# Cross-covariance attention: Q and K of five units loaded as 8 KB rows, with masked copies of Q

## The chip, the cores and the metric

The kernel runs on one core of a Trainium2 chip. Its time is the device time of one execution in microseconds (us), 127.44 at the median of three runs (127.34 to 127.64). A core has five engines with queues of their own: TensorE (PE, with its weight loads shown apart as PEld), VectorE (DVE), ScalarE (ACT), GpSimd (POOL) and SyncE (SP, which here only issues transfers). Sixteen DMA engines move data between HBM and the on-chip memory SBUF, which has 128 partitions; matrix products land in PSUM.

## The reference

Batch 8, 12 heads, 512 positions, dimension 64, all float32. Q and K are normalised along the positions, their 64 x 64 product goes through a softmax, and V is multiplied by it:

```python
Q_norm = Q / (np.linalg.norm(Q, axis=-2, keepdims=True) + 1e-10)
K_norm = K / (np.linalg.norm(K, axis=-2, keepdims=True) + 1e-10)
attn = np.einsum('bhnd,bhne->bhde', Q_norm, K_norm)
attn = np.exp(attn - np.max(attn, axis=-1, keepdims=True))
attn = attn / (np.sum(attn, axis=-1, keepdims=True) + 1e-10)
return np.einsum('bhnd,bhde->bhne', V, attn).astype(np.float32)
```

Each of Q, K, V and the output is 12.58 MB.

## The kernel before, in words

The 96 heads are cut into 12 units of 8 heads (`S = 12`), two units make a pair (`W = 6`). A unit's Q is one tile of 128 partitions x 2,048 floats (1 MB), and so is its K; a pair's V is two such tiles.

**How rows lie in a tile.** For Q and K (`Qf`, `Kf`, L168) a row of 16 positions of one head, 4 KB, goes to a partition: 32 partitions hold one head, 128 hold four, and the tile has two such groups side by side (`r`), so a load of a whole tile (L221) takes 256 rows of 4 KB. For V (`Vu`, L170) a row is 32 positions, 8 KB, a head has 16 partitions, and a tile is 128 rows.

**One unit.** `cast_qk` (L244) makes bf16 copies of Q and K in which the two heads of a partition lie beside each other, `square` (L249) squares them. `grams` (L258) multiplies K and Q: 64 matmuls of 32 rows by 128 columns, so that two heads share a product of 128 x 128 of which the two diagonal blocks are used. `sums` (L265) adds the squares over the partitions with 8 matmuls, `fold` (L272) and `norms` (L276) bring the sums to where they are needed, `powers` (L280) takes them to the power -1/2. `scale_k` (L286), `logits` (L290, four transposes), `scales_q` (L294, one call for each half of the partitions) and `exps` (L300) give the exponentials, `normalise` (L304) the softmax in bf16.

**One pair.** `cast_v` (L316) makes bf16 of V, `vtrans` (L321) transposes it on PE, `vcopy` (L328) copies it from PSUM, `outs` (L334) multiplies it by the softmax, and `ocopy` (L344) copies the product to an output tile, which `store` (L229) writes to HBM. The store of unit 9 is cut in four (`CUTS`, L231), of which a part of 124 rows and one of 4 rows carry 1,536 bytes a row; those of units 10 and 11 are halved (`HALF`, L233).

**The order.** Nothing is scheduled by the hardware or by the framework: `Order.run` (L100) plays the kernel through once, before it is built, with costs in us for each piece (`piece`, L397, and the calls under it), a rank for each kind of piece (`R`) and a bias for each choice of engine (`BIAS`), and so fixes the order of each engine's queue. For casts, squares and copies it also picks the engine. All loads of Q, K and V but the first two of K, and all stores, stand in SP's queue, in one order. SP issues in that order: where an issue has to wait for its buffer, all later ones wait behind it. Eight transfers can be under way at a time, since an issue also waits for the landing of the eighth before it.

**Buffers.** Seven tiles for Q and K as they come (`NB["qk"]`, L177), three for V, two each for the bf16 copies and squares, six for outputs. A load of Q or K waits until the tile seven places earlier has been cast.

Of the kernel before, what the change touches and what calls it, by code (L numbers as in the profile page):

```python
# [18 lines left out]
 'R': {'ck': 14.3601,  # L19
       'q': -46.9145,  # L20
       'sq': -4.5261,
       'sk': 21.309,
       'gr': 31.9137,
       's1': -8.269,
       'rd': 14.1273,
       'nn': -13.565,
       'pw': -22.1669,
       'kx': 16.8281,
       'lg': -36.3133,
       'qs': 14.727,  # L30
       'ex': 7.4539,
       'nm': 23.5766,
       'cv': -5.1919,
       'vt': 13.5707,
       'vc': 31.4911,
       'ou': -17.6156,
       'oc': 6.4318},
 'BIAS': {('cv', 'DVE'): 12.3272,
          ('vc', 'ACT'): 5.2627,
          ('oc', 'DVE'): 7.9654,  # L40
          ('q0', 'ACT'): -9.0842,
          ('sk', 'ACT'): 4.174,
          ('sk', 'DVE'): 5.4091,
          ('cv', 'ACT'): 0.906,
          ('cv', 'POOL'): -0.1651,
          ('ck', 'DVE'): -11.8527,
          ('ck', 'ACT'): -10.4645,
          ('ck', 'POOL'): -15.4937,
          ('oc', 'ACT'): 4.7795,
          ('sq', 'DVE'): -12.3114,  # L50
          ('sq', 'ACT'): -21.9953,
          ('q0', 'DVE'): -28.6804,
          ('q0', 'POOL'): -29.3142,
          ('vc', 'DVE'): -20.4676},
 'QK_PACE': 0.9356,
 'V_FROM': 0.0874,
 'V_PACE': 0.7666,
 'ST_LAG': 6.0835,
 'SPLIT': 3,
 'HALF': (10, 11),  # L60
 'WAKE': ('SP',),
 'CUTS': ((0, 0, 6, 0, 124), (0, 0, 6, 124, 128), (0, 6, 16, 0, 128), (1, 0, 16, 0, 128))}

D = 64
T = 32
# [86 lines left out]
def kernel(  # L152
# [13 lines left out]
    FINE = PAR["FINE"]  # L166

    Qf, Kf = (x.rearrange("b h (p t) d -> (b h p) (t d)", t=TT).rearrange("(w r e p) x -> w e p r x", r=2, e=2, p=128)  # L168
              for x in (Q, K))
    Vu = V.rearrange("b h (p t) d -> (b h p) (t d)", t=T).rearrange("(w r p) x -> w r p x", r=2, p=128)  # L170
# [9 lines left out]
    qmp = ctx.enter_context(tc.tile_pool(name="qmp", bufs=NB["qm"]))  # L180
    sqp = ctx.enter_context(tc.tile_pool(name="sqp", bufs=NB["sq"]))
# [31 lines left out]
    def load_qk(s, x, c):  # L213
        w, e = divmod(s, 2)
        if (s, x) not in qk32:
            qk32[s, x] = qp.tile([128, T, D], F32, name="qk32")
        issue = nc.scalar if (s, x) == (0, 1) and PAR["ACTQ"] else nc.sync
        o = qk32[s, x][:, cols(c)].rearrange("p t d -> p (t d)")
        i = (Qf, Kf)[x][w, e]
        if c is None:  # L220
            issue.dma_start(out=o.rearrange("p (r x) -> p r x", r=2), in_=i)  # L221
        else:
            issue.dma_start(out=o, in_=i[:, c])
# [17 lines left out]
    def heads(c):  # L241
        return slice(0, 2) if c is None else slice(c, c + 1)

    def cast_qk(eng, s, x, c):  # L244
        if (s, x) not in qkb:
            qkb[s, x] = qmp.tile([128, TT, 2, D], BF16, name="qb" if x == 0 else "kb")
        copy(eng, qkb[s, x][:, :, heads(c)], qk32[s, x][:, cols(c)].rearrange("p (r t) d -> p t r d", t=TT))

    def square(eng, s, x, c):  # L249
        if s not in sq:  # L250
            sq[s] = sqp.tile([128, 2, TT, 2, D], BF16, name="sq")
        o, i = sq[s][:, x, :, heads(c)], qkb[s, x][:, :, heads(c)]
        if eng == "ACT":
            nc.scalar.activation(o, i, AF.Square)  # L254
        else:
            nc.vector.tensor_tensor(out=o, in0=i, in1=i, op=ALU.mult)

    def grams(s):  # L258
        gram[s] = ps_g.tile([128, HU, 4, 2 * D], F32, name="gram")
        for t in range(TT):  # L260
            for h in range(HU):
                q, k = (qkb[s, x][32 * h:32 * (h + 1), t].rearrange("p r d -> p (r d)") for x in range(2))
                nc.tensor.matmul(gram[s][:, h, 0], k, q, start=(t == 0), stop=(t == TT - 1))  # L263

    def sums(s):  # L265
        st[s] = ps_l.tile([D, 4, 2 * D], F32, name="l")
        for t in range(0, TT, 4):
            for x in range(2):
                nc.tensor.matmul(st[s][32 * x:32 * (x + 1)].rearrange("p t d -> p (t d)"), hm,  # L269
                                 sq[s][:, x, t:t + 4].rearrange("p t r d -> p (t r d)"), start=(t == 0), stop=(t == TT - 4))  # L270

    def fold(s):  # L272
        s2[s] = small.tile([D, 2 * D], F32, name="s2")
        nc.vector.tensor_reduce(out=s2[s], in_=st[s].rearrange("p t d -> p d t"), axis=mybir.AxisListType.X, op=ALU.add)  # L274

    def norms(s):  # L276
        nn[s] = ps_l.tile([128, 2 * HU], F32, name="l")
        nc.tensor.matmul(nn[s], s2[s], sel, start=True, stop=True)  # L278

    def powers(s):  # L280
        ln = small.tile([128, 2 * HU], F32, name="ln")
        r12[s] = small.tile([128, 2 * HU], F32, name="r12")
        nc.scalar.activation(ln, nn[s], AF.Ln, bias=tiny[:, 0:1])  # L283
        nc.scalar.activation(r12[s], ln, AF.Exp, scale=-0.5)  # L284

    def scale_k(s):  # L286
        kqs[s] = small.tile([128, HU, 2 * D], F32, name="kqs")
        nc.vector.tensor_tensor(out=kqs[s], in0=gram[s][:, :, 0], in1=r12[s][:, HU:, None].to_broadcast([128, HU, 2 * D]), op=ALU.mult)  # L288

    def logits(s):  # L290
        for h in range(HU):
            nc.tensor.transpose(gram[s][:, h, 1], kqs[s][:, h], ident)  # L292

    def scales_q(s, r):  # L294
        if r == 0:
            ls[s] = small.tile([128, HU, D], F32, name="ls")
        half = (LO, HI)[r]
        nc.vector.tensor_tensor(out=ls[s][half], in0=gram[s][half, :, 1, half], in1=r12[s][half, :HU, None].to_broadcast([D, HU, D]), op=ALU.mult)  # L298
# [66 lines left out]
    hm = const.tile([128, 32], BF16, name="hm")  # L365
    nc.gpsimd.memset(hm, 0.0)
    own = const.tile([128, HU], F32, name="own")
    nc.vector.tensor_reduce(out=own, in_=ident.rearrange("p (h i) -> p h i", h=HU), axis=mybir.AxisListType.X, op=ALU.add)
    nc.vector.tensor_copy(hm[:, 0:HU], own)
    sel = const.tile([D, 2 * HU], F32, name="sel")  # L370
    for x in range(2):
        nc.gpsimd.tensor_copy(sel[:, HU * x:HU * (x + 1)], ident[0:D, 32 * x:32 * x + HU])
# [6 lines left out]
    def size(key):  # L379
        n = {"gr": 128, "s1": 16, "nn": 4, "lg": 8, "vt": 8, "ou": 32}[key[0]]  # L380
        return n // 2 if key[0] == "vt" and key[-1] is not None else n

    LOCK = {"ck", "q0", "sq", "sk", "nm", "cv"}
# [11 lines left out]
    CHOICE = ("ck", "q0", "sq", "sk", "cv", "vc", "oc")  # L395
# [17 lines left out]
    def uses(i):  # L413
        s, x = divmod(i, 2)
        return every("ck" if x else "q0", s)

    last = None
    for s in range(S):
        for c in parts(s):
            for x in range(2):  # L420
                key = ("l" + "qk"[x], s, c)
                piece(key, {"DMA": 2 * X if c is None else X}, uses(2 * s + x - NB["qk"]), [last],
                      PAR["QK_PACE"] * ((s + 0.5 * (c or 0)) / S), load_qk, s, x, c)
                last = key
    SM = NB["sm"]
    for s in range(S):
        for c in parts(s):
            dve, act, tt = two(c, 0.16, 0.52), two(c, 0.18, 0.84), two(c, 0.16, 0.52)
            for x, (load, cast, sqr, rank) in enumerate((("lq", "q0", "sq", "q"), ("lk", "ck", "sk", "ck"))):
                free = [("gr", s - NB["qm"])] + every(sqr, s - NB["qm"]) if s >= NB["qm"] else []  # L430
                piece((cast, s, c), {"DVE": dve, "ACT": act, "POOL": 2 * dve}, [(load, s, c)] + free, [], R[rank] + 0.01 * s, cast_qk, s, x, c)
                piece((sqr, s, c), {"DVE": tt, "ACT": act}, [(cast, s, c), back("s1", s, NB["sq"])], [], R[sqr] + 0.01 * s, square, s, x, c)
        piece(("gr", s), {"PE": 1.2}, every("ck", s) + every("q0", s) + [back("qs", s, 1, 0), back("qs", s, 1, 1)], [], R["gr"] + 0.01 * s, grams, s)
        piece(("s1", s), {"PE": 1.2}, every("sk", s) + every("sq", s) + [back("pw", s, 1)], [], R["s1"] + 0.01 * s, sums, s)
        piece(("rd", s), {"DVE": 0.69}, [("s1", s), back("nn", s, SM)], [], R["rd"] + 0.01 * s, fold, s)
        piece(("nn", s), {"PE": 0.3}, [("rd", s)], [], R["nn"] + 0.01 * s, norms, s)
        piece(("pw", s), {"ACT": 0.52}, [("nn", s), back("qs", s, SM, 0), back("qs", s, SM, 1)], [], R["pw"] + 0.01 * s, powers, s)
        piece(("kx", s), {"DVE": 0.69}, [("gr", s), ("pw", s), back("lg", s, SM)], [], R["kx"] + 0.01 * s, scale_k, s)
        piece(("lg", s), {"PE": 0.7}, [("kx", s)], [], R["lg"] + 0.01 * s, logits, s)
        for r in range(2):  # L440
            piece(("qs", s, r), {"DVE": 0.43}, [("lg", s), back("ex", s, SM)], [("qs", s, 0)] if r else [], R["qs"] + 0.01 * s, scales_q, s, r)
        piece(("ex", s), {"ACT": 0.425}, [("qs", s, 0), ("qs", s, 1), back("nm", s, SM)], [], R["ex"] + 0.01 * s, exps, s)
# [6 lines left out]
    for w in range(W):  # L449
# [9 lines left out]
        for n, (q, f) in enumerate(turns(w)):  # L459
# [3 lines left out]
            else:  # L463
                wait = [("qs", S - 1, 0), ("qs", S - 1, 1)] + ([("vc", w, *turns(w)[n - 4])] if n >= 4 and turns(w)[n - 4][1] is not None else [])
# [57 lines left out]
```

## Time and profile before

| | |
|---|---|
| median of three runs | 127.44 us (127.34 to 127.64) |
| the profiled execution | 127.3 us, span 125.2 us |
| granted PE clock, mean | 0.875 |
| busy: PE, PEld | 79.2 us (63%), 52.6 us (42%) |
| busy: DVE, ACT, POOL | 78.9 us (63%), 84.9 us (68%), 47.5 us (38%) |
| moved by DMA | 50.59 MB, mean 404 GB/s |
| read from and written to HBM | 37.75 MB, 12.58 MB |

The span runs from the first to the last event of the profiled execution; 2.1 us of its 127.3 lie around it. The profile's slices cut the span into 40 parts of 3.13 us; a digit is the busy share in tenths. The DMA row is the mean over the 16 DMA engines. The chain is followed back from the last instruction, at each step to what released it. A line of a group shows what is written and read, with shapes, the number of instructions, busy time, mean duration in ns and the idle time ahead of it. L numbers are lines of the kernel. The trace also holds a record of each DMA packet with its time and size, and of each landing: every DMA engine that took part in a transfer tells when its share is in.

### The profile page before, as it was taken

How to read it: one execution, taken by the hardware profiler on the slowest of the kernel's cores; microseconds unless marked ns; L12 is line 12 of the kernel's file. 1: busy time of each engine (PE TensorE's matmuls, PEld its weight loads, DVE VectorE, ACT ScalarE, POOL GpSimd, SP SyncE). 2: the span in 40 equal slices, each digit the busy share in tenths (PEclk: the TensorE clock that was granted, in tenths of full speed). 3: DMA queues.
4: the chain of work that ended last, by engine and by line, in shares of the span. 5: the costliest groups of instructions: out<-in, count | busy, mean ns of one | idle time of the engine just before them, and what ended most of it. 6: DMA issues, size and time to landing. Idle time of an engine off the chain costs nothing.

```text
span 125.2 us, 4066 instructions
## 1 busy us (share of the span) xinstructions
PE 79.2 (63%) x1800; PEld 52.6 (42%) x1800; DVE 78.9 (63%) x140; ACT 84.9 (68%) x116; POOL 47.5 (38%) x40
## 2 busy tenths in 40 slices
PE   0019369873598787859637798882898879941000
PEld 0024254561474475538525455461275456630000
DVE  2043475876852989987987599993799978700000
ACT  4068594784698853998799997938958697863000
POOL 3330665382627088061806925065144810000000
PEclk9999955999657999995999999999599999997555
DMA  3999999999999999999999999999999999999993
GB/s 129 399 419 431 424 411 418 427 419 415 420 424 423 420 428 408 421 414 428 410 432 424 410 421 415 429 414 420 427 428 410 416 416 414 418 408 412 415 395 154
DMA packets 11785, 50.59 MB, mean 404 GB/s; under 512 B 888, under 2 KB 1016, under 8 KB 10232
## 3 DMA queue, kind: packets, MB, share of 16 engines
q1 hardware_dynamic: 11480, 49.29, 95.8%
q10 hardware_dynamic: 288, 1.05, 2.3%
q8 instruction: 14, 0.23, 0.7%
q14 instruction: 3, 0.02, 0.0%
HBM read 37.75 MB, written 12.58 MB: 402 GB/s over the span
## 4 chain that ended last, share of the span: by engine, by line
DMA 70%; PE 9%; ACT 5%; DVE 4%; issue 2%; SPq 1%; ACTq 0%
DMA qk<-in_Q_dram 37%; DMA out_dram<-so 17%; DMA qk<-in_K_dram 16%; ACT so L207 5%; PE po L341 3%; PE gram L263 2%; PE gram L292 1%; PE vps L326 1%; DVE kqs L288 1%; DVE qb L209 1%; PE l L269 1%; DVE ab L313 1%; DVE s L274 0%; PE l L278 0%; ACT ln L283 0%
## 5 line engine op out<-in xcount | busy, mean ns | idle before, releaser
L211 POOL TENSOR_SCALAR kb<-qk 128x2048 bf16<-128x2048 f32 (+1 forms) x13 | 23.0, 1771 | 37.8 <-DMA qk<-in_K_dram 30.9
L254 ACT ACTIVATE sq<-qb 128x2048 bf16<-128x2048 bf16 (+1 forms) x13 | 23.1, 1776 | 7.8 <-DVE qb L209 7.6
L207 ACT COPY so<-po 128x512 f32<-128x512 f32 x47 | 25.6, 584 | 3.9 <-PE po L341 2.3
L211 POOL TENSOR_SCALAR vb<-v 128x1024 bf16<-128x1024 f32 x15 | 21.4, 1444 | 13.4 <-DMA v<-in_V_dram 9.6
L341 PE MATMUL po<-ab,vt 128*32 128x128 bf16 x768 | 20.2, 232 | 6.6 <-ACT so L207 2.1
L263 PE MATMUL gram<-qb,kb 32*128 32x128 bf16 x768 | 15.5, 237 | 12.3 <-DVE qb L209 8.8
L209 DVE CAST qb<-qk 128x2048 bf16<-128x2048 f32 (+1 forms) x12 | 13.7, 1143 | 11.2 <-DMA qk<-in_Q_dram 10.7
L326 PE MATMUL vps<-ident,vb 128*128 128x128 f32 x96 | 17.3, 305 | 4.7 <-POOL vb L211 2.7
L269 PE MATMUL l<-sq,hm 128*32 128x512 bf16 x96 | 18.4, 442 | 1.7 <-ACT sq L254 1.6
L263 PEld LDWEIGHTS <-kb 32*128 32x128 bf16 x768 | 13.3, 104 | 14.4 <-POOL kb L211 10.3
L341 PEld LDWEIGHTS <-vt 128*32 128x32 bf16 x768 | 13.8, 101 | 12.4 <-issue 7.9
L209 DVE COPY vt<-vps 128x1024 bf16<-128x1024 bf16 (+1 forms) x25 | 16.5, 665 | 3.4 <-PE vps L326 3.1
L207 ACT CAST vb<-v 128x1024 bf16<-128x1024 f32 x9 | 12.1, 1341 | 8.8 <-DMA v<-in_V_dram 8.6
L254 ACT ACTIVATE sq<-kb 128x2048 bf16<-128x2048 bf16 (+1 forms) x10 | 17.3, 1733 | 0.6 <-POOL kb L211 0.6
L326 PEld LDWEIGHTS vps<-ident,vb 128*128 128x128 f32 x96 | 11.2, 151 | 8.5 <-POOL vb L211 3.2
L274 DVE TENSOR_REDUCE s<-l 64x128 f32<-64x512 f32 x12 | 8.1, 677 | 6.5 <-PE l L269 6.5
L298 DVE TENSOR_TENSOR ls<-gram,r 64x256 f32<-64x256 f32 x24 | 10.1, 420 | 2.2 <-PE gram L292 1.9
L292 PE MATMUL gram<-ident,kqs 128*128 128x128 f32 x48 | 9.0, 316 | 3.5 <-DVE kqs L288 3.0
L288 DVE TENSOR_TENSOR kqs<-gram,r 128x512 f32<-128x512 f32 x12 | 8.3, 689 | 3.7 <-ACT r L284 3.1
L313 DVE TENSOR_TENSOR ab<-ex,rb 128x512 bf16<-128x512 f32 x12 | 9.3, 773 | 0.4
L269 PEld LDWEIGHTS <-hm 128*32 128x32 bf16 x96 | 5.5, 104 | 9.4 <-issue 7.4
L292 PEld LDWEIGHTS gram<-ident,kqs 128*128 128x128 f32 x48 | 5.7, 154 | 7.4 <-DVE kqs L288 6.6
(25 smaller groups left out, 40.2 us busy)
## 6 DMA issues: line engine op xcount, KB each, us to landing
v<-in_V_dram SPq DMA_DIRECT2D x12, 1024.0 KB, 19.8
qk<-in_Q_dram SPq DMA_DIRECT2D x11, 1024.0 KB, 19.8
qk<-in_K_dram SPq DMA_DIRECT2D x11, 1024.0 KB, 19.6
out_dram<-so SPq DMA_DIRECT2D x9, 1024.0 KB, 19.7
out_dram<-so SPq DMA_DIRECT2D x5, 512.0 KB, 9.4
qk<-in_K_dram ACTq DMA_DIRECT2D x2, 512.0 KB, 4.6
qk<-in_Q_dram SPq DMA_DIRECT2D x2, 512.0 KB, 6.3
out_dram<-so SPq DMA_DIRECT2D x1, 320.0 KB, 10.1
```

The source lines that it names most:

```text
L207: nc.scalar.copy(o, i)
L209: nc.vector.tensor_copy(o, i)
L211: nc.gpsimd.tensor_scalar(out=o, in0=i, scalar1=1.0, scalar2=0.0, op0=ALU.mult, op1=ALU.add)
L254: nc.scalar.activation(o, i, AF.Square)
L263: nc.tensor.matmul(gram[s][:, h, 0], k, q, start=(t == 0), stop=(t == TT - 1))
L269: nc.tensor.matmul(st[s][32 * x:32 * (x + 1)].rearrange("p t d -> p (t d)"), hm, sq[s][:, x, t:t + 4].rearrange("p t r d -> p (t r d)"), s ...
L288: nc.vector.tensor_tensor(out=kqs[s], in0=gram[s][:, :, 0], in1=r12[s][:, HU:, None].to_broadcast([128, HU, 2 * D]), op=ALU.mult)
L292: nc.tensor.transpose(gram[s][:, h, 1], kqs[s][:, h], ident)
L298: nc.vector.tensor_tensor(out=ls[s][half], in0=gram[s][half, :, 1, half], in1=r12[s][half, :HU, None].to_broadcast([D, HU, D]), op=ALU.mult)
L313: nc.vector.tensor_tensor(out=ab[s], in0=ex[s][:, :, None, :].to_broadcast([128, HU, 2, D]), in1=rb[:, :, :, None].to_broadcast([128, HU, ...
L326: nc.tensor.transpose(ps[:, n], vb[w][:, j].rearrange("p r d c -> p (r d c)").bitcast(F32), ident)
L341: nc.tensor.matmul(po[s, x][32 * h:32 * (h + 1), j].rearrange("p r d -> p (r d)"), v, ab[s][:, h].rearrange("p r d -> p (r d)"), start=Tru ...
```

## The change

Units 1 to 5 (`LONG`) get Q and K in the layout of V: 32 positions, 8 KB, to a partition, so that a head has 16 partitions and the tile holds eight heads below one another. A tile's rows come from two places in HBM and are loaded by two DMAs of 64 partitions each.

```diff
+    Ql, Kl = (x.rearrange("b h (p t) d -> (b h p) (t d)", t=T).rearrange("(w r e p) x -> w e r p x", r=2, e=2, p=4 * T // 2) for x in (Q, K))
...
+        if s in LONG:
+            for r, half in enumerate((LO, HI)):
+                issue.dma_start(out=o[half], in_=(Ql, Kl)[x][w, e, r])
+        elif c is None:
             issue.dma_start(out=o.rearrange("p (r x) -> p r x", r=2), in_=i)
```

A group of 32 partitions, the least that a matmul takes here, now holds two heads. To keep them apart, Q is copied twice, each time multiplied by a column (`par`) of ones and zeros that clears one head of each group; a matmul takes K of both heads and both copies of Q, 256 columns where there were 128. Squares of Q are taken from the float32 tile.

```diff
+    def mask_q(eng, s, r):
+        if (s, 0) not in qkb:
+            qkb[s, 0] = qmp.tile([128, 2, T, D], BF16, name="qb")
+        o, i, m = qkb[s, 0][:, r], qk32[s, 0], par[:, r:r + 1]
+        if eng == "ACT":
+            nc.scalar.activation(o, i, AF.Copy, scale=m)
+        else:
+            (nc.vector if eng == "DVE" else nc.gpsimd).tensor_scalar(out=o, in0=i, scalar1=m, scalar2=0.0, op0=ALU.mult, op1=ALU.add)
...
+                if s in LONG:
+                    o = gram[s][:, h, 0:2]
+                    q, k = qkb[s, 0][p, :, 2 * t:2 * t + 2].rearrange("p r t d -> p r (t d)"), qkb[s, 1][p, 2 * t:2 * t + 2].rearrange("p t d -> p (t d)")
...
+            o, i = sq[s, x].rearrange("p t r d -> p (t r) d"), qkb[s, 1] if x else qk32[s, 0]
```

Behind that, for these units, `sums` uses a mask of eight heads, `norms` has two matmuls, `scale_k` one call for each half of the partitions, `logits` four matmuls with a doubled identity (`eye2`) that add up the two halves, and `scales_q` one call for all partitions. The sums of Q and of K are pieces of their own for all units, and the squares of Q and of K are separate tiles, two buffers in all, so one for each operand. The bf16 copies of K have a pool of their own.

The constants grow: `head`, `par`, `both`, `eye2` on DVE, a larger `sel` on POOL. All ranks and biases of the planner are new, `HALF` is empty, so the stores of units 10 and 11 are whole:

```diff
+ 'LONG': (1, 2, 3, 4, 5),
+ 'XL': 1.2575,
+ 'HALF': (),
```

In the queues this gives: all ten masked copies on POOL; six whole casts of K on POOL and five on DVE (before, 11 of K and one of Q on POOL, ten of Q on DVE); the other six whole casts of Q on POOL; all 22 whole squares on ACT (before, 19 there and three on DVE); 35 output copies on ACT and 13 on DVE (before 47 and 1); 12 half casts of V each on ACT and POOL (before 9 and 15). SP's order starts with Q of unit 0, the first V tile, then Q and K of unit 1; the store of unit 0 stands ahead of the last twelve loads, that of unit 1 behind all loads.

## The prediction

> **What bounds the kernel now.** I read the page first: engine shares, the forty slices, the chain. No engine is busy over 68% of the span, but the DMA row stands at nine tenths or more in 38 of 40 slices, and the chain runs through DMAs for 70% of the span.
>
> ```profile
> span 125.2 us, 4066 instructions
> ...
> DMA  3999999999999999999999999999999999999993
> GB/s 129 399 419 431 424 411 418 427 419 415 420 424 423 420 428 408 421 414 428 410 432 424 410 421 415 429 414 420 427 428 410 416 416 414 418 408 412 415 395 154
> DMA packets 11785, 50.59 MB, mean 404 GB/s; under 512 B 888, under 2 KB 1016, under 8 KB 10232
> ...
> DMA 70%; PE 9%; ACT 5%; DVE 4%; issue 2%; SPq 1%; ACTq 0%
> ```
>
> What to see: 50.59 MB move at 410 to 430 GB/s from the first microseconds to the last, and 10,232 of 11,785 packets are under 8 KB. The DMA issues tell how far ahead the queue is:
>
> ```profile
> v<-in_V_dram SPq DMA_DIRECT2D x12, 1024.0 KB, 19.8
> qk<-in_Q_dram SPq DMA_DIRECT2D x11, 1024.0 KB, 19.8
> qk<-in_K_dram SPq DMA_DIRECT2D x11, 1024.0 KB, 19.6
> ```
>
> A megabyte passes in about 2.5 us (below), so 19.8 us from issue to landing means that eight transfers are always under way: tile buffers are free long before data come, and the engines wait for data, not the data for engines. Last the end, in the timeline:
>
> ```profile
> 110.46 7.35 SPq L235 DMA_DIRECT2D out_dram<-so  x4
> ...
> 111.99 1.68 ACT L207 COPY so<-po 128x512 f32<-128x512 f32 x3 [0.95 <-PE po L341]
> ```
>
> The last copy of an output ends at 113.67, yet the last store is issued only at 117.47, because it waits for an older store to land, and the trace has its landing at 124.35. Unit 11's megabyte begins to move at about 119.0 (the first landing of the store ahead); with the 1.3 us that the first small transfer takes from issue (0.74) to landing (2.06), the last copy could come 4.0 us later at no cost. So a change here is worth what it does to the DMA stream, as long as the engines stay within their cover.
>
> **The gain: longer rows.** The trace's packet records have one time for each size: 159 ns for 4,096 bytes (7,413 of the records between 8 and 112 us), 309 ns for 8,192 (1,534 of 1,536), 9 ns for a completion's 4 bytes. Each of the 16 DMA engines moves a 1 MB tile of Q or K as 16 packets of 4 KB, 16 x 159 = 2,544 ns; as 8 packets of 8 KB it is 8 x 309 = 2,472 ns, 72 ns less. Packets overlap a little (the windows give a DMA share of 1.02), so I also read elapsed time, the spacing of first landings between 10 and 99 us: 2.49 us for Q and K loads (17 of them), 2.45 for V loads, which have 8 KB rows already (9). That is 40 ns a tile. Ten tiles change (Q and K of five units): 0.72 us by packets, 0.40 by landings. I take the landings, since they are elapsed time.
>
> Ten tiles come as two DMAs instead of one, and the two stores that were halved are whole again, so there are 10 - 2 = 8 more completions: 8 x 9 = 72 ns by packets, about 40 ns with the overlap (a packet of either size takes some 4 ns less in the spacing than in its record). **Sum: 0.40 - 0.04 = 0.36 us, at most 0.65.** Below, it reaches to nothing, since no row shows a 64-row load.
>
> **What else is added, and its cover.**
>
> - Masks: 10 multiplications of 128x2048 on POOL, two where each long unit had one Q cast. The nearest rows are the POOL cast, 1,903 ns, and the strided V cast, 1,444 ns for half the elements, so 1.90 to 2.89 us each; I take 1.90, the same operation and shape. Counted by the changed program, POOL has 22 operations of 1.90, 4 of 1.05 and 12 V casts of 1.44, with small ones 65 us against 47.5. Per long unit it is two masks, two fifths of a K cast and about one V cast, 3.8 + 0.8 + 1.4 = 6.0 us, against 3 MB of loads, 7.4 us. Even at 2.89 (8.0 us) it falls some 11 us behind by unit 5 and catches up afterwards; a tile's buffer is wanted again only seven tiles (17 us) later, so nothing is refused.
> - ACT: 22 squares of 1.91, 4 of 1.05, 35 output copies of 0.584 (47 before), 12 V casts of 1.34, 12 us of exponentials and the table: 94.7 us against 84.9. Five squares now read f32; the ACT cast from f32 (1,341 ns for 1,024) bounds them at 2.68, 3.9 us more in all. From the first operand (6.5 us) to the latest harmless end (117.7) there are 111 us, so 13 to 16 stay idle.
> - DVE: five K casts of 1.23 and 12 output copies of 0.67 come, ten Q casts of 1.23, two halves of 0.73 and three squares of 1.23 go; ten half kqs for five whole, five whole ls for ten halves (0.42 to 0.69 each), and 1.4 us of constants: 76 to 80 us, against 78.9.
> - PE: 320 of 768 gram matmuls become twice as wide. The group's 15.5 us is 1.3 per unit; doubling adds 0 to 1.3 each, at most 6.5 us on an engine that is busy 67 of 89 us between 8 and 97. The constants at the start are ready long before Q's first half (landing at 6.5 us).
> - SP: eight more issues of 0.4 to 0.5 us, each against 1.2 us of transfer. That V's first tile now goes ahead of Q of unit 1 changes no byte of the stream. With eight DMAs under way and half tiles, the queue ahead shrinks from 19.8 to some 9.9 us in the long stretch. SP's longest single wait is 5.2 us (for ln); behind it in order stand all later loads, and 9.9 us still cover it. The first store now stands ahead of twelve loads; at 2.47 us a megabyte unit 0's last V tile is in by 18 us, and SP reaches this store at about 46 us, so it holds up nobody.
> - The squares of a unit now have one buffer per operand instead of two: a square waits for the previous unit's column sums, behind which other work of ACT queues. That is inside ACT's 13 idle microseconds.
>
> All of this costs nothing while the DMA queue stays full. If the cover goes, each late microsecond beyond 4.0 at the end, or beyond 9.9 in the long stretch, is paid in full.
>
> **The rivals.**
>
> *Half rate for 64 rows (slower).* Each long load fills only half of the partitions. If two DMA engines then share a way into SBUF, or half of the engines stand still, a packet takes 618 ns: 20 loads x 4 packets x 309 ns = 24.7 us more, 152. It decides from the first long load; engines that drift apart (landings of one load spread over 1.6 us from 24 us on) would soften it to perhaps 140. Against idle engines: the store of 124 rows has landings on 4 engines, those of 128 and of 16 rows on 16, so 64 should take 16. Against a shared way: that same store gives each of four engines 31 rows, most of which other engines read for the stores about it. The 128 packets of 1,536 bytes (its own, and those of the four rows left) ran between 114 and 117 us and all took 65 ns, and 461 of 467 packets of 4 KB from 112 to 118 us took their usual 159. That is reading of SBUF, though; no row shows two engines writing there. [...] Chance 0.14.
>
> *ACT becomes the bound (slower).* It is the engine with the least to spare: 9.7 to 13.6 us more work, to be put where it was idle (26 us of the same 111). It decides once more than 4.0 us of that work finds no gap. If half of it finds none, 4.9 to 6.8 us, the end comes 0.9 to 2.8 us later than the forecast, 127.9 to 129.8. For it: in the trace ACT's largest idle times end with a V load (8.6 us) or a cast (7.6), and gaps that wait for data can be too early to be used. Against it: the planner's order puts 12 more output copies on DVE. Chance 0.09.
>
> *The gain is given back (no change).* Twenty starts of 512 KB instead of ten of 1 MB, or another spread of the engines at the end: in the last store the 16 landings lie 2.9 us apart, and the end is the latest. The trace's halved stores pass at 1.25 us each, 2.50 a megabyte against 2.49, so a split costs 0.01 to 0.02 a tile; a late engine could cost 0.3. Result 127.2 to 127.7. Chance 0.15.
>
> **How the numbers follow.** The profiled execution took 127.3 (span 125.2 and 2.1 around it); the median of three is 127.44. Less 0.36 that is 126.94 and 127.08; I give 127.0. The forecast has 0.62; its own range is 126.3 (0.65 and a better end) to 127.3. The 80% range takes in the second and third rivals and leaves out the first: 126.2 to 129.0. About 0.2% (0.25 us) is what a measurement can tell from no change. Faster by more: 0.55 of the forecast's 0.62. Within: its other 0.07 and 0.10 of the third rival, 0.17. Slower: 0.14 + 0.09 + 0.05 = 0.28.
>
> **What would show it.** Right: packets under 8 KB fall from 10,232 to about 7,800 (2,560 of 4 KB go, 8 x 16 completions come); 8 KB packets of Q and K at 309 ns; DMA slices still at nine from 5 to 115 us and 420 GB/s or a little over in slices 4 to 15; ACT's last copy well before 117.7. Wrong: 8 KB packets at 400 to 620 ns and slices 4 to 15 at 220 to 350 GB/s (first rival); a dip in the DMA row together with a long SP wait for ACT or POOL (second).

## The result

The changed kernel takes 153.88 us at the median of six runs (152.96 to 155.15), the kernel before 127.39 beside it (127.31 to 127.64): 1.209 times as long, 95% interval 1.203 to 1.215. The rival of half rate came true, close to the 152 us worked out for it. In the experiments some kernels scatter from one execution to the next; ratios compare undisturbed executions, medians are over all.

The page of the profile after (155.15 us, the longest of the six): span, the DMA rows of the 40 slices (3.84 us each now), the chain, and one row of issues (how many, size, median us to landing).

```profile
span 153.4 us, 4176 instructions
...
DMA  4999999999999999999999999999999999999981
GB/s 169 401 371 218 226 378 310 233 218 226 218 303 226 233 216 235 320 295 201 243 419 409 419 425 424 419 419 413 423 414 429 414 411 418 413 417 410 414 366 77
DMA packets 10634, 50.60 MB, mean 330 GB/s; under 512 B 1016, under 2 KB 1144, under 8 KB 7800
...
DMA 82%; ACT 4%; PE 3%; issue 2%; SPq 1%; DVE 0%
...
qk<-in_Q_dram SPq DMA_DIRECT2D x12, 512.0 KB, 20.3
```

The DMA row alone shows nothing: it stands at nine tenths as before. Busy means that packets are under way, not that they are fast. The row under it tells: from slice 4 to slice 20 the rate is 201 to 243 GB/s where only Q and K of the long units pass, 295 to 378 where a V load lies between, and 409 to 429 from then on to the end of the stream. 7,800 packets under 8 KB is the number that the prediction counted, so the change does what it says. The two windows say the same in sums; the columns are window, length, busy time of each engine with its instructions, clock, DMA share, GB/s. After:

```profile
10.00:62.00 52.00, 33.24 (x486) 20.63 (x486) 21.46 (x34) 26.36 (x30) 26.00 (x15) 0.80 1.02 249
```

and before, in the same window:

```profile
10.00:62.00 52.00, 39.54 (x799) 26.38 (x788) 37.60 (x63) 38.66 (x50) 25.77 (x16) 0.84 1.02 420
```

PE, DVE and ACT did less in these 52 us than before, since data came later; only POOL did the same. Packets of 8 KB between 30 and 40 us took 593 ns at the mean and 515 at least; V's, and all of them behind the stretch, take 309 at the median. Half loads land 2.34 us apart, and 2.4 to 2.5 behind a V load, where 1.24 was expected; all twenty take 47.7 us instead of 24.8, 22.9 more. Three smaller terms stand beside it. The five V loads in between lose 1.4 (the longest gap ahead of one is 3.54 us, not 2.45). The sixteen landings of one load drift apart, to 6.5 us at 73 us, and the first 4 KB load behind the stretch lands 4.5 us after the one before it, 2.0 more than a megabyte's 2.49. At the end they still lie 4.85 us apart in the last store, where they lay 2.91 apart before, and the end is the latest: 1.9. The sum, 28.2, is all by which the span is longer (153.4 against 125.2).

### The profile page after: what moved, and what is told of

Its sections match the earlier page's. It is cut to its first block, busy times and chain, and to the rows that moved or that the text cites. A ratio compares the mean times of both kernels' runs of the same rounds, so it can differ in the third digit from the quotient of the medians.

```text
span 153.4 us, 4176 instructions
## 1 busy us (share of the span) xinstructions
PE 89.7 (58%) x1830; PEld 59.9 (39%) x1830; DVE 81.1 (53%) x148; ACT 88.7 (58%) x110; POOL 64.8 (42%) x54
## 4 chain that ended last, share of the span: by engine, by line
DMA 82%; ACT 4%; PE 3%; issue 2%; SPq 1%; DVE 0%
DMA qk<-in_Q_dram 32%; DMA v<-in_V_dram 23%; DMA out_dram<-so 14%; DMA qk<-in_K_dram 13%; ACT so L216 3%; PE po L397 2%; PE vps L382 1%; DVE vt L218 0%; PE gram L345 0%; SPq L231 0%; SPq L408 0%; ACT r L327 0%; ACT ln L326 0%; SPq L239 0%
## 5 line engine op out<-in xcount | busy, mean ns | idle before, releaser
L275 POOL TENSOR_SCALAR qb<-qk,par 128x2048 bf16<-128x2048 f32 x10 | 19.6, 1976 | 19.9 <-DMA qk<-in_Q_dram 14.5
L300 PE MATMUL gram<-qb,kb 32*128 32x128 bf16 (+1 forms) x768 | 23.4, 286 | 4.3 <-DVE kb L218 4.2
L216 ACT COPY so<-po 128x512 f32<-128x512 f32 x35 | 19.2, 582 | 6.8 <-PE po L397 5.5
L220 POOL TENSOR_SCALAR qb<-qk 128x2048 bf16<-128x2048 f32 (+1 forms) x8 | 14.0, 1748 | 21.3 <-PE gram L300 11.9
L285 ACT ACTIVATE sq<-qb 128x2048 bf16<-128x2048 bf16 (+1 forms) x8 | 13.5, 1692 | 6.2 <-POOL qb L220 4.9
L313 DVE TENSOR_REDUCE s<-l 128x128 f32<-128x512 f32 (+1 forms) x12 | 8.2, 687 | 16.2 <-PE l L308 16.2
L220 POOL TENSOR_SCALAR kb<-qk 128x2048 bf16<-128x2048 f32 (+1 forms) x8 | 13.5, 1688 | 2.7 <-DMA qk<-in_K_dram 2.7
L218 DVE CAST kb<-qk 128x2048 bf16<-128x2048 f32 x5 | 6.1, 1227 | 14.7 <-DMA qk<-in_K_dram 14.7
L369 DVE TENSOR_TENSOR ab<-ex,rb 128x512 bf16<-128x512 f32 x12 | 13.5, 1122 | 0.4
L285 ACT ACTIVATE sq<-qk 128x2048 bf16<-128x2048 f32 x5 | 9.5, 1904 | 5.7 <-DMA qk<-in_Q_dram 5.7
L218 DVE COPY so<-po 128x512 f32<-128x512 f32 x13 | 8.7, 685 | 3.7 <-PE po L397 3.5
## 6 DMA issues: line engine op xcount, KB each, us to landing
v<-in_V_dram SPq DMA_DIRECT2D x12, 1024.0 KB, 19.8
```

The costliest lines, as they stand in the source:

```text
L216: nc.scalar.copy(o, i)
L218: nc.vector.tensor_copy(o, i)
L220: nc.gpsimd.tensor_scalar(out=o, in0=i, scalar1=1.0, scalar2=0.0, op0=ALU.mult, op1=ALU.add)
L275: (nc.vector if eng == "DVE" else nc.gpsimd).tensor_scalar(out=o, in0=i, scalar1=m, scalar2=0.0, op0=ALU.mult, op1=ALU.add)
L300: nc.tensor.matmul(o, k, q, start=(t == 0), stop=(t == TT - 1))
L313: nc.vector.tensor_reduce(out=s2[s], in_=st[s].rearrange("p (t d) -> p d t", d=d), axis=mybir.AxisListType.X, op=ALU.add)
```

## The experiments

### Loads by themselves

Theory: 64 rows to partitions 0 to 63, or 64 to 127, move at half rate because DMA engines share ways into SBUF. Rival: the source is at fault (rows from two places, half a megabyte a load). Eleven stages of nothing but transfers:

```diff
+    # C: 64 rows of 8 KB, partitions 32 to 95
+    for n in range(16):
+        nc.sync.dma_start(out=x[32:96, n], in_=Q8[64 * n:64 * n + 64])
```

> Loads and stores alone, no attention is computed; each stage moves 8 MB or less and ends before the next begins. Stages: A 128 rows of 8 KB; B 64 rows to partitions 0-63 and 64-127 in turn, as in the changed kernel; C 64 rows to partitions 32-95; D 64 rows to 0-63 only; E as B, but the source takes every second 8 KB row; F as B, with the second half issued from ACT's queue; G 128 rows of two 4 KB parts; H 32 rows to 0-31 and 64-95 in turn; then stores of 128 rows, of 64 rows in turn, and from 32-95. Port theory (the 16 DMA engines reach only half of the ways into SBUF when the target is one half of the partitions): A and C 309 ns a packet and about 425 GB/s; B, D, E about 590 ns and 225 GB/s; F between, since an engine can have packets of both halves at hand; H like B. Source theory (16 engines read one 512 KB piece of HBM at a pitch of 32 KB and get in each other's way there): C as slow as B, E faster than B or at least different, stores not slower. Both: G about 420 GB/s. Stores: the prediction's reading of the 1,536-byte packets says that reading 64 partitions costs nothing, 420 GB/s in all three; if the ports limit reading as well, the 64-row stores in turn take 225 GB/s and those from 32-95 420.

Windows inside five stages (the last column is GB/s): 128 rows; halves 0 to 63 and 64 to 127 in turn; 32 to 95; 0 to 63 alone; one half from SP's queue, the other from ACT's.

```profile
10.00:20.00 10.00, 0.00 (x0) 0.00 (x0) 1.00 1.02 428
30.00:55.00 25.00, 0.00 (x0) 0.00 (x0) 1.00 1.02 220
72.00:82.00 10.00, 0.00 (x0) 0.00 (x0) 1.00 1.01 424
95.00:125.00 30.00, 0.00 (x0) 0.00 (x0) 1.00 1.01 206
180.00:205.00 25.00, 0.00 (x0) 0.00 (x0) 1.00 1.02 259
```

The second and third window differ in nothing but the partitions: 64 rows of 8 KB a load, the same rows of HBM in the same order, 16 DMA engines, one queue, and 220 against 424 GB/s (packets of 603 and 318 ns). With every second row of the source the halves stayed at 2.39 us a load and 604 ns, so the source falls. 32 rows (0 to 31 and 64 to 95 in turn) gave 234 GB/s, no less than 64. **Stores** of 64 rows passed at full rate: 1.23 us per 512 KB and 315 ns a packet (282 to 288 us), against 2.46 us a megabyte and 310 ns for 128 rows. So halves in turn are slow when SBUF is written and not when it is read; no run stored from one half alone.

### The split alone

The kernel before, with its 4 KB rows, its order and its work, but with the loads of units 1 to 5 in two halves:

```diff
+        if s in (1, 2, 3, 4, 5):
+            for half in (LO, HI):
+                issue.dma_start(out=o[half].rearrange("p (r x) -> p r x", r=2), in_=i[half])
-        if c is None:
+        elif c is None:
```

> The kernel before, with one thing changed: Q and K of units 1 to 5 are loaded by two DMAs of 64 partitions each, in the old layout of 4 KB rows. No masks, no other order. Port theory and source theory: the whole loss, 4 KB packets at about 300 ns in those loads and 151 to 154 us. Work theory (masks, wider products, the new order): 127.4 to 127.8, as splitting costs only ten more completions.

Measured: 156.06 us (154.63 to 156.63), ratio 1.222 (1.218 to 1.226), packets of 4 KB at 302 ns. The page's GB/s row:

```profile
GB/s 179 398 214 223 290 381 215 229 307 222 221 224 231 223 285 216 233 233 226 364 418 423 416 423 434 403 420 423 415 421 425 418 412 419 414 411 421 410 369 60
```

The same valley without masks, wide products or 8 KB rows. The split by itself is the whole loss; the rest of the change took back about 2 us at the medians (156.06 against 153.88).

### No split

The change with one load of 128 rows of 8 KB per tile; the wrong heads then lie beside each other.

```diff
-            for r, half in enumerate((LO, HI)):
-                issue.dma_start(out=o[half], in_=(Ql, Kl)[x][w, e, r])
+            issue.dma_start(out=o, in_=(Qu, Ku)[x][w, e])
```

> The changed kernel, but Q and K of units 1 to 5 are loaded by one DMA of 128 rows of 8 KB each, from eight consecutive heads; these are other heads than V's, so the output of those units is not the reference's, while all work stays. Port theory and source theory: the loss is gone, and what the prediction reckoned for the longer rows shows: 0.3 to 0.7 us under the kernel before, 126.7 to 127.1. Work theory: 150 or more stays.

Measured: 127.17 to 135.38 us in twelve executions, nine of them above 131, ratio 0.9997 (0.9983 to 1.0011) from the other three. The loss is gone, but the gain of 0.36 us does not appear. The profiled execution (127.52) shows what stands in its way, in the chain and the DMA rows of its page:

```profile
DMA  4999999999999999999999999999999999999992
GB/s 140 400 427 435 422 430 422 433 420 427 425 430 425 422 410 421 433 409 407 379 426 422 416 425 410 421 418 421 421 429 409 418 412 416 416 420 348 403 412 117
...
DVE 41%; PE 27%; ACT 14%; issue 6%; DMA 4%; POOL 1%; SPq 0%; DVEq 0%
```

The chain is no longer one of transfers: DMA has 4% of it. ACT's last copy of an output ends at 118.2, where it ended at 113.67 before, and the prediction put the latest harmless end at 117.7. Slices 20 and 37 dip to 379 and 348 GB/s. The cover of 4.0 us is used up even in this execution, one of the three shortest. The gain itself is there: the ten long loads land 2.46 us apart at the mean, where 4 KB loads took 2.49 before.

### Which partitions meet

Two engines with two rows of 64 KB, to chosen pairs of partitions, and other sets of rows:

```diff
+        nc.sync.dma_start(out=x[0:64:32, 8 * n:8 * n + 8].rearrange("p a x -> p (a x)"), in_=Qw[2 * n:2 * n + 2])
```

> Loads alone again, nothing is computed. A: the half loads of the changed kernel in turn, but behind one load of 40 rows on the eight lowest engines, which puts those 1.2 us behind. If the engines collide in fixed pairs, one of the lower and one of the upper eight, A runs near full rate from then on (about 1.25 to 1.5 us a half); if all 16 share one limit, 2.39 us stay. B: 56 rows to partitions 0-55, which eight engines carry. Port theory: half of the engines carry nearly as much as 16 did, some 190 to 215 GB/s, with 8 KB packets of 309 to 350 ns. [...] E to H: two rows of 64 KB on two engines, to partitions 0 and 4, 0 and 32, 0 and 64, 0 and 1. [...] Source theory: all four alike.

In the second of two loads, partitions 0 and 4 took 2,418 ns for the 64 KB, 0 and 64 too; 0 and 1 took 5,125 ns, 0 and 32 too, 2.12 times as long. Rows to partitions 0 to 15 took 1,202 ns for each 8 KB, four times 309 less a little. By the theory of shared ways, partition 0 has one with 1 and with 32 and not with 4 or 64, and four engines share one in the load of 16 rows. That is an estimate from these times: no record shows a way. Windows of two stages: halves in turn, and 64 rows to every second partition.

```profile
10.00:40.00 30.00, 0.00 (x0) 0.00 (x0) 1.00 1.01 218
84.00:96.00 12.00, 0.00 (x0) 0.00 (x0) 1.00 1.01 425
```

A first trial of engines out of step was inconclusive: its odd transfer, which went by ten engines and not eight, was over 0.5 us after the half loads began. 56 rows went by fourteen engines (642 ns, about 180 GB/s), not eight.

### Engines out of step

The prediction hoped that engines that drift apart would soften a shared way. Two kernels held up eight engines, or one, two and four, behind the eighth half load of a stream:

```diff
+            if n == 8 and k:
+                nc.sync.dma_start(out=y[0:32:4, 0:k], in_=V32[0:8, 0:k])
```

> DMAs alone; the output is not the reference's. Three stages, each of 24 loads of 64 rows of 8 KB to partitions 0 to 63 and 64 to 127 in turn from SP's queue. Stage A has nothing else. In stages B and C one transfer of eight rows (to partitions 0, 4, 8 to 28, so eight DMA engines take one row each) stands behind the eighth load: rows of 32 KB in B, 16 KB in C. Then twelve loads and twelve stores of 128 rows for scale. [...] Theory (engines meet only while they write the same half): A stays at 2.39 us a load throughout; in B the eight engines that carry the 32 KB rows fall a whole half load behind the other eight (4 packets of 8 KB at 309 ns, 1.24 us), so that from then on one eight writes the upper half while the other writes the lower, and the loads behind come every 1.25 us at packets of 310 ns. In C they fall half a load behind and meet half of the time: packets between 310 and 600 ns, loads every 1.6 to 2.4 us. Rival (any two of the sixteen engines that write 64 rows slow each other, or the limit is one of the stream's as a whole): B and C go on at 2.39 us a load, 600 ns a packet, behind the odd transfer.

> DMAs alone; the output is not the reference's. Three stages of 24 loads of 64 rows of 8 KB, to partitions 0 to 63 and 64 to 127 in turn, as in m3_phase_shift, where eight engines fell a whole load behind and nothing got faster. Behind the eighth load stands one transfer that holds up fewer engines: 17 rows of 2 KB in stage A (one engine), two rows of 32 KB in B (two engines), four in C (four engines). Theory (two engines share a way into SBUF, and those that met in m3 both belonged to the eight that were delayed): an engine that falls a load behind its partner writes the other half, and both go at 310 ns a packet as long as they stay apart: two engines of sixteen in A. In B it is two if engine pairs are 0-1, and four if they are farther apart; in C none if pairs lie within the first four engines, and eight if not. The others stay at 600 ns. Rival (the limit is one of the stream, not of pairs): all sixteen stay at 600 ns in every stage. Spacing of loads by last landing: 2.39 us by both, since the slowest engines set it.

Windows behind the odd transfer, first with eight engines late by a 32 KB row, then with one engine late:

```profile
89.00:100.00 11.00, 0.00 (x0) 0.00 (x0) 1.00 1.01 218
```

```profile
28.00:40.00 12.00, 0.00 (x0) 0.00 (x0) 1.00 1.02 220
```

The landings of one load then lie 2.7 us apart in the first and 2.5 in the second, a whole half load, and yet none of the 293 packets of the first window took less than 551 ns, and none of the 416 from 24.5 to 40 us in the second less than 520. Two and four late engines gave the same (531 and 532 at least). The theory that two engines slow each other only while they write the same half has fallen: a half load kept half rate with its engines out of step in every way tried. What holds up an engine that has its half to itself is open; the rival of the two runs, a limit of the stream as a whole, agrees with both, but does not say which part sets it.

### The split without the loss

The kernel before with the halves as even and odd partitions:

```diff
+            for n in range(2):
+                issue.dma_start(out=o[n:128:2].rearrange("p (r x) -> p r x", r=2), in_=i[n:128:2])
```

> The kernel before with the loads of units 1 to 5 split in two 64-row DMAs as in the run that split them alone (4 KB rows, no masks, old order), but one takes the even rows into the even partitions and the other the odd ones. Same number of DMAs, rows, bytes and packets as there. [...] If a load of 64 rows is slow as such, or if a split disturbs the queue, 150 and more stay.

Measured: 128.25 us (128.23 to 128.28), ratio 1.0066 (1.0053 to 1.0079), packets at 160 ns. The GB/s row keeps 404 to 438 through the long stretch but for one slice:

```profile
GB/s 144 395 327 416 434 417 417 430 411 419 419 424 420 420 438 404 415 413 429 411 429 425 412 422 413 437 404 420 433 419 417 409 416 413 417 412 417 412 377 96
```

In slice 3 (327) the first half load lands 1.98 us after Q's last half of unit 0, and from there on all landings are some 0.65 us late, which is most of the 0.84 us. Twenty starts of half a megabyte cost the other 0.2 at most; the one gap while the queue is still short costs more.

The changed kernel with even and odd partitions, masks and sums adapted, first with its own ranks, then with those of the kernel before:

```diff
-            for r, half in enumerate((LO, HI)):
-                issue.dma_start(out=o[half], in_=(Ql, Kl)[x][w, e, r])
+            for r in range(2):
+                issue.dma_start(out=o[r:128:2], in_=(Ql, Kl)[x][w, e, r])
```

> The changed kernel with its two half loads going to the even and to the odd partitions instead of the lower and the upper 64; masks, head sums and the scaling of K follow that layout, the planner's numbers and order are its own. Port theory: the loads run at full rate and the kernel behaves as the run with eight consecutive heads did, 127.1 to 127.6 in its best executions and 131 to 135 in others, since the order leaves the engines no cover. If the half loads cost something else, 140 or more.

> The same layout on even and odd partitions, with the ranks, biases and paces of the kernel before and its halved last stores. If the planner's new numbers were what took the cover away (they cost 7.5 us without long units), the forecast's gain shows: 126.8 to 127.2 in all executions. If the added work of ACT and POOL took it, times scatter between 127 and 135 again.

The first took 127.19 us in its profiled execution (131.2 to 134.9 in five others, no ratio), with 8 KB packets at 310 ns; the second 127.11 to 134.75, ratio 1.0047 (0.9991 to 1.0103). Neither beats the kernel before: the valley is gone, and the engines set the end in its place (DMA has 4% of the chain in both). With the old ranks too the gain stays away, so the new ranks alone did not take it. In the first, ACT's last copy begins at 117.7, and SP's longest waits are for ACT's copies (line, engine waited for: us in total, times, longest):

```profile
SPq L249 <- ACT so L216: 15.3, 4, 9.9
```

### What takes the cover

The change without long units, so with its new ranks on the old work; the unsplit change without the second mask; and with narrow products:

```diff
- 'LONG': (1, 2, 3, 4, 5),
+ 'LONG': (),
```

```diff
+        if r:
+            return
```

```diff
+                if s in LONG and 0 < t < TT - 1:
+                    o = gram[s][:, h, 0]
```

> The changed kernel with no long unit at all (the list of long units is empty): the new ranks and biases, the separate sums of Q and K, the smaller buffers of squares, whole last stores, but 4 KB rows, no masks, no wide products. If the planner's new numbers by themselves cost nothing, 127.2 to 127.6. If the new order is at fault in part, 129 to 135.

> The run with eight consecutive heads (128-row loads), with the second masked copy of Q left out: the wide matmuls read the first copy twice, so heads are mixed and the output of units 1 to 5 is not the reference's. [...]

> e2_eight_heads (the change with a single load of 128 rows of 8 KB, so with the wrong heads beside each other), where in units 1 to 5 only the first and last of the sixteen steps of the product take both masked copies (256 columns); the fourteen between take the first alone (128 columns, as the kernel before), so the second half of each product is incomplete. Both masked copies are still made, so POOL, ACT and DVE have the same work as in e2. If the wider products on PE are what takes the engines' cover when the granted clock is low (nine of twelve executions of e2 at 131.1 to 135.4 with clocks of 0.83 to 0.87), most executions come at 127.1 to 127.7, whatever their clock. [...] Without the second mask (e3_one_mask) it was seven of twelve at 127.1 to 127.7.

With no long unit: 135.84 us, ratio 1.062 (1.059 to 1.066). The ranks belong to the new work, and on the old one SP stands for an output copy so long that the stream runs dry (the profiled execution, at 138.64 us the longest of five):

```profile
DMA  4999999999999999999999999999999400796991
```

```profile
SPq L249 <- ACT so L216: 28.3, 5, 20.8
```

One wait of 20.8 us is longer than the 19.8 us of transfers ahead of it, and slices 32 to 35 are what is left. Without the second mask: ratio 0.9995 (0.9984 to 1.0005), no gain either. With narrow products: 134.7 us, ratio 1.056 (1.051 to 1.062), though PE has less to do than in the unsplit change. This settles nothing on wide products: all six executions took 132.3 to 141.2 us, but nine of the unsplit change's twelve took 131.1 to 135.4 too, and the profiled one had a granted clock of 0.84 against 0.95 (its products of K and Q took 17.6 us of PE, 20.8 there). Which of the added operations uses up the cover is not settled.

## Why the prediction was wrong, step by step

- **What bounds the kernel** was right: the stream of transfers, and so a rate that halves for 20 loads goes into the end in full: 22.9 us by the half loads themselves, 5.3 by V loads, drift and the last store, 28.2 of the span.
- **The step that failed** is the weighing of half rate: "that is reading of SBUF, though; no row shows two engines writing there", and then a chance of 0.14 all the same. So the sum charged a half load nothing but its completion, 0.04 us for all, where the twenty cost 22.9, and the rival's 152 stayed outside a range that ended at 129.0. The row set against a shared way was a store, of 124 rows, and stores in halves turn out to be free of the limit (315 ns a packet for 64 rows, where loads took 603). A row of the other direction excludes nothing. Measured for loads were 220 GB/s in halves and 428 whole; on this the trace of before was silent. That 152 comes so near the measured time is in part luck: it had 24.7 us for the half loads and none of the 5.3 beside them.
- **"Perhaps 140" by drift** was wrong: half loads stayed at 2.34 us although landings had drifted 6.5 us apart, and lateness put in on purpose changed nothing. Drift went with a further loss, 2.0 us behind the stretch and 1.9 at the end.
- **The gain of 0.36 us** was right in its terms and did not show: 8 KB packets do take 309 to 310 ns where loads keep their rate (V's, and the long units' by even and odd partitions), and whole long loads land 2.46 us apart, but the best executions without the loss lie at 127.1 to 127.5, as before.
- **Sizes of the added work** were close, but for PE and ACT. Two rows of before, then those after, by group:

```profile
L263 PE MATMUL gram<-qb,kb 32*128 32x128 bf16 x768 | 15.5, 237 | 12.3 <-DVE qb L209 8.8
L313 DVE TENSOR_TENSOR ab<-ex,rb 128x512 bf16<-128x512 f32 x12 | 9.3, 773 | 0.4
```

```profile
L275 POOL TENSOR_SCALAR qb<-qk,par 128x2048 bf16<-128x2048 f32 x10 | 19.6, 1976 | 19.9 <-DMA qk<-in_Q_dram 14.5 <-PE gram L300 5.4
L285 ACT ACTIVATE sq<-qk 128x2048 bf16<-128x2048 f32 x5 | 9.5, 1904 | 5.7 <-DMA qk<-in_Q_dram 5.7
L300 PE MATMUL gram<-qb,kb 32*128 32x128 bf16 (+1 forms) x768 | 23.4, 286 | 4.3 <-DVE kb L218 4.2
L369 DVE TENSOR_TENSOR ab<-ex,rb 128x512 bf16<-128x512 f32 x12 | 13.5, 1122 | 0.4
```

A mask takes 1.98 us (1.90 predicted, 2.89 as a bound), a square from float32 1.90 (the bound of 2.68 was far off), POOL 64.8 us (65). PE's products grew by 7.9 us, where at most 6.5 was allowed (in the unsplit change, at a clock of 0.95, by 5.3). ACT was busy 88.7 us, 3.8 more than before and not 9.8: the prediction's 94.7 is a sum of durations, which the trace after confirms (94.6), but it stood against a busy time (84.9) in which overlapping instructions count once; their sum before is 91.9.
- **"All of this costs nothing"** was wrong, though hidden by the larger loss. It was summed by engine, and the last row is what such a sum can't see: the same instruction `ab` took 1,122 ns at the mean against 773 before, with a least of 691 in both traces, so DVE stood in it. What it waited for is in the times: the three of the twelve that began while POOL had an operation under way ended 0.53 to 0.54 us behind it, after 2,357 to 2,444 ns; the other nine took 691 to 694. The unsplit change has three such too, and its five casts of K on DVE took 8.7 us where 6.1 is their time in the changed kernel, while POOL was busy 69.0 us against 47.5 before. Its last copy ends 0.5 us past the cover, more than the 0.36. That is the second rival's mechanism (engines instead of transfers), with DVE and PE at the head of the chain and ACT third.

## What to carry to other kernels

Before a load is cut by partitions, time the parts by themselves: here 64 rows to the low and the high half in turn passed at 220 GB/s, to partitions 32 to 95 at 424, to every second partition at 425. Read the GB/s row beside the DMA row, since a stream at half rate looks busy (a DMA share of 1.02 at 220 GB/s). Evidence from stores said nothing of loads here (426 GB/s against 220 for 64 rows in turn), a sum of durations is not to be set against a busy time (94.7 us against 84.9), and cover that was counted engine by engine overstated what was free (DVE stood 1.7 us behind POOL, three times).

## What was not expected of the hardware

- The limit has a direction: loads of 64 rows into the two halves in turn pass at 220 GB/s, while stores of the same shape pass at 1.23 us per 512 KB (426 GB/s).
- Two halves from two queues (SP's and ACT's) pass at 259 GB/s, more than from one (220) and far from 424. Against one half alone (206) that is 26% more, and halves in turn from one queue are 7% more.
- A lag of a whole half load between the DMA engines, for one, two, four or eight of them, left every packet at 520 ns or more.
- A DVE multiply (`ab`) that began during a POOL operation of 1.90 to 1.98 us ended 0.53 to 0.54 us behind it, so it took 2,357 to 2,444 ns where 691 to 694 is its time, about 1.7 us more in all three cases.
